# One of eight channel tiles of a depthwise convolution moved from TensorE tap matmuls to VectorE multiply-adds

## The chip, the cores and the metric

The kernel runs on one core of a Trainium2 chip. A core has five engines with a queue of instructions each: TensorE (PE; the loading of its stationary operand is shown apart, as PEld), VectorE (DVE), ScalarE (ACT), GpSimd (POOL) and SyncE (SP), which here only issues DMAs. Engines run independently; within one queue the order is fixed when the kernel is built, and an instruction that waits holds up what stands behind it. The metric is the device time of one execution in microseconds (us). Of the kernel before, three runs gave 2607.24, 2607.55 and 2607.57 us: median 2607.55.

## The reference, cut to what matters

The program is an encoder of four layers over 512 positions and 1024 channels, in float32. Layers 0 and 3 mix positions with a convolution module, layer 1 with neighbourhood attention, layer 2 with retention; a gated conv-FFN follows each. Only the convolution module is touched:

```python
def conv_module(h, w_in, b_in, dw_w, dw_b, ln_g, ln_b, w_out):
    a, gt = jnp.split(h @ w_in + b_in, 2, axis=-1)
    u = a * jax.nn.sigmoid(gt)
    u = dwconv(u, dw_w, dw_b)
    u = layernorm(u, ln_g, ln_b)
    return jax.nn.silu(u) @ w_out
```

`dwconv` is depthwise, 31 taps wide and centred: output position t of channel c is the bias of c plus the sum over k = 0..30 of `dw_w[k, c] * u[t + k - 15, c]`, with zeros beyond the ends. No channel sees another, so each of the eight tiles of 128 channels can be made in its own way. The layernorm behind it needs mean and variance over all 1024 channels of a position.

## The kernel before

**Precision.** Every product is made on TensorE from a high and a low part (`split`, L163, and `split_w`, L146: ScalarE casts the high part to fp32r, VectorE subtracts it from the source to get the low part). A matrix product is three matmuls, high by high, high by low, low by high (`mm3`, L153, its matmuls at L154 to L156).

**Layout.** The residual stream lies as 8 tiles `x[k]` of 128 channels by 512 positions. Weights are streamed: SP issues the load of a raw tile `wr`, then it is split into `wh` and `wl` (three buffers each). PSUM has eight banks; the convolution takes four as pool `psa` (the two input products) and four as `psb` (the taps and the transposes).

**The convolution** (`conv`, L349) runs per channel tile m = 0..7.

- `front(m)` (L370) makes the two halves of the input product, 48 matmuls; VectorE scales both by the row norm (L392, L394), ScalarE applies the sigmoid (L393), and VectorE writes the gated product `u` (L396), de-interleaved by position modulo 4 into one of two tiles `us`. POOL then issues four copies (L401), which gather 32 channels by 4 position phases onto 128 partitions as `xf`; `split` makes `X` from it (high and low).
- `taps(m, X, half)` (L406) makes 64 of the 128 channels as two blocks of 32. Per block a banded matrix of the tap weights `wraw` of 576 KB is loaded by SP (L413), split into `W` (three buffers; ScalarE L164, VectorE L165), and 9 pairs of matmuls follow: one 256 columns wide (L419) and one 128 wide (L422). A channel tile has four blocks, so 36 pairs. VectorE adds bias and both parts into `y` (L431, L434), which lies by position on the partitions and by channel along the free axis.
- Four groups of `bn_stats` (`BNG`, L63, L439), each issued when the last of its channels is there, gather the layernorm's statistics; behind the last of them 23 matmuls whose result is not used stand on TensorE (L444), then `norm(k)` (L469) normalises `y`, transposes it back (L482) and the output product follows.

**Order.** The program is written as a software pipeline (L448): step m traces `front(m)`, then the second half of tile m - 2's taps, then the first half of tile m - 1's. The text is not the final order. A planner simulates all engines with a cost estimate for each instruction and gives each queue its order from that; where several instructions are ready, the earlier-traced one goes first, as far as the trace shows. In the steady part TensorE runs 40 front matmuls, three tap blocks, 8 front matmuls, one tap block, and so on. What sets when something can run is therefore its data and buffers, then its place in the text.

**Start.** For the first convolution the weights of `front(0)` (input tiles 0 and 8) are loaded with the input `x`, in parts (L989), and its two banks come from `psb`.

Of the kernel before, what the change touches and what calls it, by code (L numbers as in the profile page):

```python
# [8 lines left out]
F32 = mybir.dt.float32  # L9
# [8 lines left out]
P = 128  # L18
T = 512
# [4 lines left out]
CW = 31  # L24
FT = 22
FC = 3
# [6 lines left out]
_n = 0  # L33
for _name, _w in (
    ("n1g", 32), ("n2g", 32), ("cbin", 32), ("clg", 16), ("clb", 16), ("qg", 1), ("kg", 1), ("gng", 16), ("logd", 8),
    ("fdw", 4 * 44 * FC), ("fdb", 4 * 44),
):
    COLS[_name] = _n
    _n += _w
# [11 lines left out]
SH = 4  # L51
# [8 lines left out]
NRAW = 2  # L60
HPO = 100000
NQZ = 2
BNG = ((0, 8), (8, 14), (14, 15), (15, 16))  # L63
NWARM = 23


@with_exitstack
def tile_trunk(
# [17 lines left out]
    def nm(s):  # L86
        uid[0] += 1
        return f"{s}{uid[0]}"
# [152 lines left out]
    def stats2():  # L241
        ps = bank(psb)
        bcast(rstd_col, ps)
        nc.scalar.copy(rstd_bc, ps)
# [104 lines left out]
    def conv(j, after):  # L349
        with ExitStack() as st:  # L350
# [8 lines left out]
            with ExitStack() as s2:  # L359
                up = s2.enter_context(tc.tile_pool(name=nm("cvu"), bufs=1, reuse_waits=RW))  # L360
                dp = s2.enter_context(tc.tile_pool(name=nm("cvd"), bufs=2, reuse_waits=RW))
                us = [up.tile([P, SH, QL], F32, tag=f"u{i}", name=nm("u")) for i in range(2)]
                for u in us:
                    nc.vector.memset(u[:, :, :4], 0.0)
                    nc.vector.memset(u[:, :, QL - 4:], 0.0)
# [2 lines left out]
                    nc.vector.tensor_copy(ap, sqacc[:, :1])  # L368

                def front(m):  # L370
                    where = psb if early and m == 0 else psa
                    pa, pg = bank(where), bank(where)
                    ws = state.pop("first", None) if m == 0 else None
                    if ws:
                        for k in range(KD):
                            s = slice(k * P, (k + 1) * P)
                            for ps, (wh, wl) in zip((pa, pg), ws):
                                mm3(ps, wh[:, s], wl[:, s], xhi[k], xlo[k], k == 0, k == KD - 1)
                        after_squares(bias[:, :1])
                        nc.scalar.dma_start(bias, cdb[j])  # L380
                        stats1()
                        stats2()
                    else:
                        for (ps, c) in ((pg, m + 8), (pa, m)):
                            wh, wl = load_w(cw_in[j, c], D)
# [3 lines left out]
                            if m == 0:  # L389
                                stats2() if c == 0 else stats1()  # L390
                    ta, tg = t512(), t512()
                    nc.vector.tensor_tensor(tg, pg, rstd_bc, MUL)  # L392
                    nc.scalar.activation(tg, tg, AF.Sigmoid, bias=pc("cbin", j * 16 + 8 + m))  # L393
                    nc.vector.tensor_tensor(ta, pa, rstd_bc, MUL)  # L394
                    u = us[m % 2]
                    state["u"] = nc.vector.scalar_tensor_tensor(  # L396
                        u[:, :, 4:4 + P], ta.rearrange("p (q s) -> p s q", s=SH),
                        pc("cbin", j * 16 + m), tg.rearrange("p (q s) -> p s q", s=SH), ADD, MUL)
                    xf = dp.tile([P, 4, QL], F32, tag="xf", name=nm("xf"))
                    for b in range(4):  # L400
                        nc.gpsimd.dma_start(xf[:, b, :], u[32 * b:32 * b + 32])  # L401
                    X = dp.tile([P, 4, 2, QL], F32R, tag="X", name=nm("X"), bufs=3)
                    split(xf, X[:, :, 0, :], X[:, :, 1, :])
                    return X

                def taps(m, X, half):  # L406
                    ps = bank(psb)
# [25 lines left out]
                            bb[:, b].unsqueeze(1).broadcast_to([P, SH, nb, 32]), ADD)  # L433
                        nc.vector.tensor_tensor(yv[:, :, b], pv[:, 0, :, b], t[:, :, b], ADD)  # L434
                    c1 = m * 2 + half + 1
                    for n, (a0, a1) in enumerate(BNG):
                        if c1 == a1:
                            for r in range(SH):
                                nc.vector.bn_stats(bst[:, r, n, :], y[:, r, a0 * 64:a1 * 64])  # L439
                    if c1 == 16:  # L440
# [4 lines left out]
                        with tc.issue_after(state["cast"].ins):  # L445
                            nc.scalar.activation(sm(1), zero, AF.Silu)

                fr = {}  # L448
                for m in range(10):
                    if m < 8:  # L450
                        fr[m] = front(m)
                    if m >= 2:
                        taps(m - 2, fr[m - 2], 1)
                    if 1 <= m <= 8:
                        taps(m - 1, fr[m - 1], 0)
            mv = sm(8)
            for r in range(SH):
                nc.vector.bn_aggr(mv[:, 2 * r:2 * r + 2], bst[:, r])
# [579 lines left out]
def _layout(inp):  # L1038
# [28 lines left out]
    put("logd", np.repeat(f["ret_log2_inv_decay"].reshape(1, 8), P, 0))  # L1067
    put("fdw", f["ffn_dw_w"].reshape(4, FC, 44, P).transpose(3, 0, 2, 1).reshape(P, -1))
    put("fdb", cols(f["ffn_dw_b"]))

    half = 128
    theta = (np.float32(1.0) / (np.float32(10000.0) ** np.linspace(0.0, 1.0, half, dtype=np.float32))).astype(np.float32)
# [71 lines left out]
```

## Time and profile before

| what | value |
|---|---|
| median of three runs | 2607.55 us |
| the profiled execution's own time | 2606.53 us |
| its span, first to last instruction | 2604.8 us |
| mean granted TensorE clock | 1.000 |
| busy: PE / PEld / DVE / ACT / POOL | 2591.2 / 2154.2 / 1641.6 / 1052.8 / 235.0 us |
| first convolution, first front to last taps and norm | about 20 to 172 us of the span |
| second convolution, the same | about 2021 to 2180 us |

Busy time of an engine is the union of its instructions' records, so that matmuls that overlap in the pipeline are counted once; their mean duration is longer than the distance from one to the next. The chain of waits is followed back from the last instruction to what released each step. In a group of instructions the columns are line, engine, operation, output <- inputs by the program's names, shapes and count; then busy us and mean ns of one; then idle us of the engine just before them and what ended it. In a table by stretch of time an engine's busy us stands with its count of instructions in brackets.

### The profile page before, as it was taken

The numbers are of one execution on the slowest core, as the hardware profiler recorded it, in microseconds if no ns is written. First come the engines' busy times: TensorE is split into PE (matmuls) and PEld (weight loads), VectorE is DVE, ScalarE is ACT, GpSimd is POOL, SyncE is SP. The second block draws the span as 40 slices with busy tenths as digits, with TensorE's granted clock in tenths as the row PEclk, the third lists the DMA queues.
The fourth block names the chain that finished last, engine by engine and source line by source line (L and its number), as shares of the span: only waits on it lengthen the run. The fifth ranks groups of instructions, "written<-read, shape, count | busy, mean of one in ns | idle before, by whom it ended". The sixth has DMA issues, their size and how long they took to land.

```text
span 2604.8 us, 32584 instructions
## 1 busy us (share of the span) xinstructions
PE 2591.2 (99%) x12886; PEld 2154.2 (83%) x12886; DVE 1641.6 (63%) x2640; ACT 1052.8 (40%) x1431; POOL 235.0 (9%) x253
## 2 busy tenths in 40 slices
PE   9999999999999999999999999999999999999999
PEld 7988888889998888888888888888888888788888
DVE  6777777437878777634656566677733667677732
ACT  5444444335655444323333333444422445444421
POOL 1104000003421100000000000100000101100000
PEclk9999999999999999999999999999999999999999
DMA  6624222333232222333221221222233651222232
GB/s 235 222 92 162 90 96 96 90 98 117 82 93 82 97 93 93 93 97 109 73 89 65 89 73 65 97 98 89 95 91 110 228 192 69 92 97 96 89 109 79
DMA packets 79785, 275.12 MB, mean 106 GB/s; under 512 B 10080, under 2 KB 13024, under 8 KB 79632
## 3 DMA queue, kind: packets, MB, share of 16 engines
q1 hardware_dynamic: 74304, 259.18, 30.5%
q0 software_dynamic: 4032, 11.14, 1.5%
q10 hardware_dynamic: 1296, 2.72, 0.3%
q8 instruction: 101, 1.65, 0.3%
q14 instruction: 52, 0.43, 0.1%
HBM read 263.04 MB, written 5.63 MB: 103 GB/s over the span
## 4 chain that ended last, share of the span: by engine, by line
PE 98%; DVE 1%; DMA 1%; ACT 0%; issue 0%; POOL 0%; SPq 0%; DVEq 0%; POOLq 0%
PE ps L155 27%; PE ps L154 27%; PE ps L156 27%; PE ps L419 3%; PE ps L160 3%; PE ps L161 3%; PE ps L159 3%; PE ps L422 1%; PE ps L311 1%; PE ps L312 1%; PE ps L316 1%; PE ps L664 1%; PE ps L444 0%; DMA x<-in_xT 0%; PE ps L482 0%
## 5 line engine op out<-in xcount | busy, mean ns | idle before, releaser
L149 ACT CAST wh<-wr 128x1024 fp32r<-128x1024 f32 (+1 forms) x410 | 424.1, 1036 | 1083.8 <-PE ps L155 791.0
L155 PE MATMUL ps<-xl,wh 128*128 128x512 f32 x1856 | 736.4, 397 | 0.3 <-DVE xl L213 0.3
L156 PE MATMUL ps<-xh,wl 128*128 128x512 f32 x1856 | 733.4, 395 | 0.1
L154 PE MATMUL ps<-xh,wh 128*128 128x512 f32 x1856 | 730.8, 394 | 1.7 <-DVE t L392 1.1
L150 DVE TENSOR_TENSOR wl<-wr,wh 128x1024 fp32r<-128x1024 f32 (+1 forms) x407 | 494.9, 1216 | 337.9 <-ACT wh L149 335.3
L154 PEld LDWEIGHTS ps<-xh,wh 128*128 128x128 f32 x1856 | 348.4, 188 | 88.9 <-DVE t L392 1.3
L155 PEld LDWEIGHTS ps<-xl,wh 128*128 128x128 f32 x1856 | 348.5, 188 | 83.9 <-DVE xl L213 0.6
L156 PEld LDWEIGHTS ps<-xh,wl 128*128 128x128 f32 x1856 | 348.3, 188 | 81.7 <-DVE wl L150 0.5
L154 PE MATMUL ps<-hh,wh 128*128 128x512 f32 (+1 forms) x726 | 281.7, 388 | 0.5 <-DVE x L341 0.5
L155 PE MATMUL ps<-hl,wh 128*128 128x512 f32 (+1 forms) x726 | 281.6, 388 | 0.0
L156 PE MATMUL ps<-hh,wl 128*128 128x512 f32 (+1 forms) x726 | 281.6, 388 | 0.0
L277 DVE TENSOR_TENSOR t<-ps,rstd_bc 128x512 f32<-128x512 f32 x176 | 120.9, 691 | 158.5 <-PE ps L156 158.5
L231 POOL TENSOR_TENSOR sqacc<-t,sqacc 128x512 f32<-128x512 f32 x49 | 75.2, 1534 | 1261.9 <-ACT t L226 1261.4
L154 PEld LDWEIGHTS ps<-hh,wh 128*128 128x128 f32 x726 | 136.5, 188 | 31.3 <-DVE x L341 0.7
L155 PEld LDWEIGHTS ps<-hl,wh 128*128 128x128 f32 x726 | 136.5, 188 | 30.7
L156 PEld LDWEIGHTS ps<-hh,wl 128*128 128x128 f32 x726 | 136.5, 188 | 30.6
L160 PE MATMUL ps<-wl,xh 128*128 128x256 f32 (+1 forms) x512 | 159.2, 312 | 0.6 <-DVE wl L150 0.6
L161 PE MATMUL ps<-wh,xl 128*128 128x256 f32 (+1 forms) x512 | 159.2, 312 | 0.0
L159 PE MATMUL ps<-wh,xh 128*128 128x256 f32 (+1 forms) x512 | 158.5, 312 | 0.0
L280 ACT ACTIVATE t<-t,par 128x512 f32<-128x512 f32 x176 | 142.7, 815 | 6.0 <-DVE t L277 5.9
L284 DVE SCALAR_TENSOR_TENSOR t<-t,par,t 128x511 f32<-128x511 f32 x176 | 132.2, 751 | 5.5
L419 PE MATMUL ps<-W,X 128*128 128x256 f32 x576 | 134.2, 331 | 0.9 <-DVE W L165 0.9
(236 smaller groups left out, 3481.9 us busy)
## 6 DMA issues: line engine op xcount, KB each, us to landing
wr<-in_f_up SPq DMA_DIRECT2D x176, 512.0 KB, 3.3
wraw<-in_cdw SPq DMA_DIRECT2D x64, 576.0 KB, 4.7
wr<-in_f_down SPq DMA_DIRECT2D x64, 448.0 KB, 3.3
wr<-in_f_down SPq DMA_DIRECT2D x32, 512.0 KB, 3.5
wr<-in_cw_in SPq DMA_DIRECT2D x30, 512.0 KB, 4.0
wr<-in_nat_qkv SPq DMA_DIRECT2D x24, 512.0 KB, 3.3
wr<-in_cw_out SPq DMA_DIRECT2D x16, 512.0 KB, 3.4
wr<-in_ret_qk SPq DMA_DIRECT2D x16, 512.0 KB, 3.3
```

The costliest lines, as they stand in the source:

```text
L149: nc.scalar.copy(hi[:, :n], raw[:, :n])
L150: eng.tensor_tensor(lo[:, :n], raw[:, :n], hi[:, :n].bitcast(F32), SUB)
L154: nc.tensor.matmul(o, wh, ah, start=first, stop=False)
L155: nc.tensor.matmul(o, wh, al, start=False, stop=False)
L156: nc.tensor.matmul(o, wl, ah, start=False, stop=last)
L159: nc.tensor.matmul(o, ah, wh, start=first, stop=False)
L160: nc.tensor.matmul(o, ah, wl, start=False, stop=False)
L161: nc.tensor.matmul(o, al, wh, start=False, stop=last)
L277: nc.vector.tensor_tensor(u, ps, rstd_bc, MUL)
L280: nc.scalar.activation(a, u, AF.Identity, bias=pc("fdb", l * 44 + c), scale=pt[:, w + 1:w + 2])
L284: nc.vector.scalar_tensor_tensor(a[:, :T - 1], u[:, 1:], pt[:, w + 2:w + 3], a[:, :T - 1], MUL, ADD)
L419: nc.tensor.matmul(o, X[:, b, 0, a:a + P], W[:, a].rearrange("p h n -> p (h n)"), start=a == 0, stop=False)
```

## The change

Channel tile 6 (`CD`) of each of the two convolutions gets another way from `u` to `y`.

- Its gated product is written dense, with 15 zero columns on either side, into a new tile `ud`. It needs no copies by POOL and no `X`.
- `direct(k0, k1)` makes the taps on VectorE: for k = 0 one `tensor_scalar` (times the weight, plus the bias), then 30 `scalar_tensor_tensor` (`ud` shifted by k, times the weight of tap k, plus `yd`, in place). Weights and bias come as one column each from the parameter table `par`, which grows by 64 columns.
- When all 31 are traced, four TensorE transposes with a stride of four positions turn `yd` into the layout of `y`, and ScalarE copies them there.
- The order of the tiles becomes 6, 0, 1, 2, 3, 4, 5, 7, so tile 6 goes first. `CTAPS` spreads the 31 instructions over the steps of the pipeline: 0, 3, 5, 5, 5, 5, 5, 3, 0, 0. The taps of the other seven tiles start one step later, in step 2, and there is one tile fewer of them.
- What was tied to tile 0 as the first front (early weights, banks, statistics) is tied to tile 6, and the second group of `bn_stats` (channels 512 to 895) is issued behind tile 5's taps.

```diff
-BNG = ((0, 8), (8, 14), (14, 15), (15, 16))
+BNG = ((0, 8, 8), (8, 14, 12), (14, 15, 15), (15, 16, 16))
 NWARM = 23
+CD = 6
+CORDER = (CD, 0, 1, 2, 3, 4, 5, 7)
+CTAPS = (0, 3, 5, 5, 5, 5, 5, 3, 0, 0)
...
+                ud = up.tile([P, T + CW - 1], F32, tag="ud", name=nm("ud"))
+                yd = up.tile([P, T], F32, tag="yd", name=nm("yd"))
+                nc.vector.memset(ud[:, :CW // 2], 0.0)
+                nc.vector.memset(ud[:, T + CW // 2:], 0.0)
...
-                    where = psb if early and m == 0 else psa
+                    where = psb if early and m == CD else psa
...
+                    if m == CD:
+                        nc.vector.scalar_tensor_tensor(
+                            ud[:, CW // 2:CW // 2 + T], ta, pc("cbin", j * 16 + m), tg, ADD, MUL)
+                        return None
                     u = us[m % 2]
...
+                def direct(k0, k1):
+                    for k in range(k0, k1):
+                        w = pc("cwd", j * CW + k)
+                        if k == 0:
+                            nc.vector.tensor_scalar(yd, ud[:, :T], w, pc("cbd", j), MUL, ADD)
+                        else:
+                            nc.vector.scalar_tensor_tensor(yd, ud[:, k:k + T], w, yd, MUL, ADD)
+                    if k0 < k1 == CW:
+                        ps = bank(psb)
+                        yr = yd.rearrange("p (q r) -> p r q", r=SH)
+                        for r in range(SH):
+                            nc.tensor.transpose(ps[:, r * P:(r + 1) * P], yr[:, r], ident)
+                        nc.scalar.copy(y[:, :, CD * P:(CD + 1) * P],
+                                       ps.rearrange("p (r c) -> p r c", r=SH))
...
-                fr = {}
-                for m in range(10):
-                    if m < 8:
-                        fr[m] = front(m)
-                    if m >= 2:
-                        taps(m - 2, fr[m - 2], 1)
-                    if 1 <= m <= 8:
-                        taps(m - 1, fr[m - 1], 0)
+                fr, done = {}, 0
+                for n in range(10):
+                    if n < 8:
+                        fr[n] = front(CORDER[n])
+                    direct(done, done + CTAPS[n])
+                    done += CTAPS[n]
+                    if n >= 3:
+                        taps(CORDER[n - 2], fr[n - 2], 1)
+                    if 2 <= n <= 8:
+                        taps(CORDER[n - 1], fr[n - 1], 0)
...
-        for c in (0, 8):
+        for c in (CD, CD + 8):
```

More of the change, by code (lines that the diff above doesn't have):

```diff
@@ L35 @@
     ("n1g", 32), ("n2g", 32), ("cbin", 32), ("clg", 16), ("clb", 16), ("qg", 1), ("kg", 1), ("gng", 16), ("logd", 8),
-    ("fdw", 4 * 44 * FC), ("fdb", 4 * 44),
+    ("fdw", 4 * 44 * FC), ("fdb", 4 * 44), ("cwd", 2 * CW), ("cbd", 2),
 ):
@@ L370, in front @@
                 def front(m):
-                    where = psb if early and m == 0 else psa
+                    where = psb if early and m == CD else psa
                     pa, pg = bank(where), bank(where)
-                    ws = state.pop("first", None) if m == 0 else None
+                    ws = state.pop("first", None) if m == CD else None
                     if ws:
@@ L388, in front @@
                                 mm3(ps, wh[:, s], wl[:, s], xhi[k], xlo[k], k == 0, k == KD - 1)
-                            if m == 0:
-                                stats2() if c == 0 else stats1()
+                            if m == CD:
+                                stats2() if c == m else stats1()
                     ta, tg = t512(), t512()
@@ L394, in front @@
                     nc.vector.tensor_tensor(ta, pa, rstd_bc, MUL)
+                    if m == CD:
+                        nc.vector.scalar_tensor_tensor(
+                            ud[:, CW // 2:CW // 2 + T], ta, pc("cbin", j * 16 + m), tg, ADD, MUL)
+                        return None
                     u = us[m % 2]
@@ L435, in taps @@
                     c1 = m * 2 + half + 1
-                    for n, (a0, a1) in enumerate(BNG):
-                        if c1 == a1:
+                    for n, (a0, a1, at) in enumerate(BNG):
+                        if c1 == at:
                             for r in range(SH):
@@ L1069, in _layout @@
     put("fdb", cols(f["ffn_dw_b"]))
+    cd = slice(CD * P, (CD + 1) * P)
+    put("cwd", f["conv_dw_w"][:, :, cd].transpose(2, 0, 1).reshape(P, -1))
+    put("cbd", f["conv_dw_b"][:, cd].T)
     half = 128
```

## The prediction

> **What bounds the kernel now.** I read the page first: busy times and the chain of waits.
>
> ```profile
> span 2604.8 us, 32584 instructions
> ...
> PE 2591.2 (99%) x12886; PEld 2154.2 (83%) x12886; DVE 1641.6 (63%) x2640; ACT 1052.8 (40%) x1431; POOL 235.0 (9%) x253
> ...
> PE 98%; DVE 1%; DMA 1%; ACT 0%; issue 0%; POOL 0%; SPq 0%; DVEq 0%; POOLq 0%
> ```
>
> TensorE sets the end: 98% of the chain, and only 13.6 us of the span without it. Work taken from TensorE is therefore worth its full time, unless TensorE then waits. Whether it would is a matter of the two stages touched, so next I read the table by stretch: both convolutions, then one steady period of the second (48 front matmuls and 36 tap pairs).
>
> ```profile
> core 0: us, PE busy (x) PEld busy (x) DVE busy (x) ACT busy (x) POOL busy (x), PEclk, DMA share, GB/s
> ...
> 20.00:172.00 152.00, 150.86 (x943) 134.04 (x943) 109.76 (x173) 68.79 (x71) 17.46 (x32) 1.00 0.60 202
> ...
> 2021.00:2180.00 159.00, 158.06 (x974) 139.77 (x973) 109.13 (x165) 68.53 (x71) 17.41 (x32) 1.00 0.55 183
> ```
>
> ```profile
> 2084.40:2103.87 19.47, 19.47 (x123) 17.29 (x122) 12.49 (x14) 7.99 (x8) 2.16 (x4) 1.00 0.59 189
> ```
>
> TensorE is busy throughout at a granted clock of 1.00, VectorE for 72% (109.76 of 152) and 64% of the period. That is the room into which the change puts work. The waits of TensorE, first convolution and then second, each show one that concerns fronts or taps:
>
> ```profile
> PE ps L154 <- DVE t L392: 1.1, 1, 1.1
> ```
>
> ```profile
> PE ps L419 <- DVE W L165: 0.9, 1, 0.9
> ```
>
> The second is the tail: tile 7, the last, has to go through product, copies and splits before its taps. The chain in order of time shows it:
>
> ```profile
> 2152.39 0.70 DVE t L394
> ...
> 2153.18 1.16 DVE u L396
> ...
> 2154.62 1.62 POOL xf L401 x3
> 2156.25 1.91 issue
> ...
> 2158.17 4.28 DMA xf<-u
> ...
> 2162.47 0.66 ACT X L164
> ...
> 2163.80 0.42 DVE y L434
> 2164.22 1.37 DVE W L165
> ...
> 2165.63 0.38 PE ps L419
> ```
>
> From 2152.39 to 2165.63 TensorE lives on six tap blocks of earlier tiles (12.4 us by the price below), then waits.
>
> **Removed from TensorE.** At the end of the first convolution TensorE makes ten tap blocks in one run:
>
> ```profile
> 145.26:165.94 20.68, 20.68 (x90) 16.77 (x89) 1.00 0.29 97
> ...
> 145.26:165.94 20.68, 19.91 (x90) 17.21 (x90) 1.00 0.29 97
> ```
>
> These are the records of L419 and of L422 in that stretch, 90 each, so 10 blocks of 9 pairs in 20.68 us, 2.07 us each. A tile has four: 8.27 us. Two convolutions: **-16.54 us**. The mean durations on the page overlap in the pipeline and can't be added up:
>
> ```profile
> L419 PE MATMUL ps<-W,X 128*128 128x256 f32 x576 | 134.2, 331 | 0.9 <-DVE W L165 0.9
> ```
>
> **Added to TensorE.** Four transposes per convolution. The chain has a run of 16 in the retention stage; the group of L482 has their duration one by one:
>
> ```profile
> 1320.51 1.75 PE ps L890 x16
> ```
>
> ```profile
> L482 PE MATMUL ps<-ident,yn 128*128 128x128 f32 x64 | 11.2, 279 | 0.1
> ```
>
> 1.75 / 16 = 0.109 us each in a run, so 8 of them cost 0.87 us. The new ones read their source with a stride of four positions, which no row shows: from 0.109 if the load still hides behind the matmul ahead, to 0.279 each (2.23 in all) if none overlaps. I take 0.109, the pace of a run, as they too stand in one: **+0.87 us**. Net -15.67.
>
> The Trainium skill ("TensorE: Matmul & The Clock Gate", Part 4: PE-mode transpose) puts a transpose at about 275 ns in the context of a kernel, most of it access latency. The row's 279 ns agrees as a duration, but the run of 16 shows that it is not the distance between two. By the page's figure the eight would cost 2.2 us, and the net would be -14.3.
>
> **Added to VectorE.** Per convolution 31 instructions over 512 elements. Their likeness is the FFN's pair that adds a shifted tile times a column into an accumulator in place:
>
> ```profile
> 402.69 0.75 DVE L282 SCALAR_TENSOR_TENSOR t<-t,par,t 128x511 f32<-128x511 f32 x1
> 403.47 0.75 DVE L284 SCALAR_TENSOR_TENSOR t<-t,par,t 128x511 f32<-128x511 f32 x1
> ```
>
> The second needs the first's result and starts 0.78 us after it. So 31 x 0.78 = 24.2 us per convolution; the first of them, a `tensor_scalar`, has no row of its form and is priced alike (0.8 us or less, it moves nothing).
>
> **Removed from VectorE**, by the groups of the steady period and of the first convolution:
>
> ```profile
> L165 DVE TENSOR_TENSOR W<-wraw,W 128x1152 fp32r<-128x1152 f32 x4 | 5.4, 1358 | 1.2 <-ACT W L164 1.2
> ...
> L396 DVE SCALAR_TENSOR_TENSOR u<-t,par,t 128x512 f32<-128x512 f32 x1 | 1.1, 1141 | 0.1
> L434 DVE TENSOR_TENSOR y<-ps,t 128x256 f32<-128x256 f32 x2 | 0.8, 425 | 0.1
> L431 DVE TENSOR_TENSOR t<-ps,bias 128x256 f32<-128x256 f32 x2 | 0.8, 422 | 0.3 <-PE ps L422 0.3
> L165 DVE TENSOR_TENSOR X<-xf,X 128x544 fp32r<-128x544 f32 x1 | 0.7, 718 | 0.0
> ...
> L394 DVE TENSOR_TENSOR t<-ps,rstd_bc 128x512 f32<-128x512 f32 x1 | 0.7, 692 | 3.5 <-PE ps L156 3.5
> ```
>
> Four `W` splits (5.4), one `X` split (0.7), two evacuations into `y` (1.7), and the dense product in place of the de-interleaved one (1.14 to 0.75, as L282): 8.2 us. Net +16.0, so in the first convolution 109.76 + 16.0 = 125.8 us in 152 - 7.8 = 144.2 us: **87%**. A steady period gets five of them, 12.49 + 3.9 = 16.4 of 19.47. VectorE doesn't become the bound by its sum.
>
> **Whether it comes late.** What TensorE needs of VectorE in time is `W`, with three buffers: when a block ends, ScalarE casts the next but two and VectorE splits it, while TensorE has two blocks left, 4.14 us.
>
> ```profile
> L164 ACT CAST W<-wraw 128x1152 fp32r<-128x1152 f32 x64 | 73.9, 1159 | 64.6 <-PE ps L422 58.8 <-issue 2.9 <-DMA wraw<-in_cdw 2.3
> ```
>
> 1.16 + 1.36 = 2.52 us, so a slack of 1.6 us. One or two of the new instructions ahead of a split (0.78, 1.56) cost nothing; three cost 0.7 us, five 2.3 us. They wait for nothing but `ud` and their predecessor, so the planner can put them into VectorE's idle stretches from the first front on (3.5 us before each L394 in the period above): the first convolution's stretch has 152 - 109.76 = 42.2 us idle, and the net of 16.0 is wanted. I expect them to be done well before their last place in the text.
>
> **The ends.** Start: tile 0's `X` is now that of the second front. Before, in the first convolution, VectorE's rows at the start were:
>
> ```profile
> 38.20 0.68 DVE L394 TENSOR_TENSOR t<-ps,rstd_bc 128x512 f32<-128x512 f32 x1
> ...
> 52.20 0.73 DVE L165 TENSOR_TENSOR X<-xf,X 128x544 fp32r<-128x544 f32 x1 [1.31 <-ACT X L164]
> ```
>
> ```profile
> 52.85 0.28 PE L419 MATMUL ps<-W,X 128*128 128x256 f32 x1
> ```
>
> The second `X` was split by 52.9 us, and TensorE, with fronts until then, took its first tap at 52.85. A fourth front can now stand there, since the second's banks were read by 38.9 us. Nothing is lost. Tail: between the last front and tile 7's taps stood (5,1), (6,0), (6,1), now (4,1), (5,0), (5,1): six blocks as before, so the wait of 0.9 us stays. In the first convolution the same chain had little left:
>
> ```profile
> 154.91 0.72 DVE L165 TENSOR_TENSOR X<-xf,X 128x544 fp32r<-128x544 f32 x1 [0.36 <-ACT X L164]
> 155.55 0.42 DVE L434 TENSOR_TENSOR y<-ps,t 128x256 f32<-128x256 f32 x1
> 155.96 2.63 DVE L165 TENSOR_TENSOR W<-wraw,W 128x1152 fp32r<-128x1152 f32 x2
> ```
>
> Tile 7's first `W` was ready at 155.96 + 1.36 = 157.3, wanted at 145.26 + 6 x 2.07 = 157.7. One new instruction in front there would cost 0.4 us, in the second convolution 0.8; a few more in the middle may cost some tenths. For all waits together I take **+1.0 us**, between -2.0 (both waits of before vanish) and +4.2 (three in a row, 0.7 us, in six of the twelve periods).
>
> **At no cost.** ScalarE loses four casts of `W` and one of `X` (5.3 us) and gets one copy out of PSUM; POOL loses four copies and SP four loads of 576 KB; none sets the end. The copy's likeness:
>
> ```profile
> L244 ACT COPY rstd_bc<-ps 128x512 f32<-128x512 f32 x7 | 4.1, 584 | 6.6 <-PE ps L190 6.6
> ```
>
> It holds up a cast behind it by 0.6 us, inside the slack of 1.6; without that cover it costs 0.6 us per convolution. The four `bn_stats` of the second group keep their place among the taps. The 64 columns more of `par` (33 KB, beside 576 KB of each load saved) lie behind `x` on SP's queue, and the first that reads anything of that load is the sigmoid of the first front, once the row norm is there.
>
> **The sum.** 2606.53 (the profiled execution's own time) - 16.54 + 0.87 + 1.0 = 2591.9. The median stands 1.0 above the profiled run: **2592.9 us**, range of this case alone -2.0 to +4.2 in place of +1.0: 2589.9 to 2596.1. By the skill's price of the transposes it would be 2594.2.
>
> **Rivals.**
>
> *Splits come late, by a little.* The planner reckons the new instructions too cheap or groups them by three ahead of a `W` split in every period: 12 x 0.7 = 8.4 us of waits. 2607.55 - 15.67 + 8.4 = 2600.3 us. For it: VectorE at 87% serves in fixed order. Against: the slack, and the idle stretches during the fronts' 11 us.
>
> *The cover of the tail goes.* TensorE, with less work, uses up two of the six blocks before the last front is through, and waits 4.14 us for tile 7's `X` in each convolution: +8.3, 2600.2 us. For it: 0.4 us left there and 0.9 missing. Against: the count of blocks is the same, and fronts stand ahead of taps in the text.
>
> *Slower: the groups of `CTAPS` go as they are traced,* five in a row (3.9 us) ahead of a split that TensorE needs next, because they stand before that step's taps in the text. Each costs 2.3 us, a group of three 0.7: per convolution 5 x 2.3 + 2 x 0.7 = 12.9, in all 25.8: 2617.7 us. The point from which it is slower: 7.8 us of waits per convolution, that is 1.3 us in each of six periods, or four in a row each time. Against: the first groups are ready while TensorE runs fronts alone, and the chain once begun needs no wait.
>
> That the change doesn't do what it says I see no way for: 72 of 576 pairs are not issued.
>
> **How the numbers follow.** Forecast 0.70; splits a little late 0.11; tail 0.08; groups as traced 0.11. A measurement tells no change from about 0.2%, 5.2 us, so no change is 2602.3 to 2612.8. The forecast, the tail and 0.08 of the small delays are faster: 0.86. No change: 0.03 of the small delays and 0.04 of the groups' milder part: 0.07. Slower: 0.07. Range: 2589 (a little under the case's lower end, as orders elsewhere may shift) to 2601, which takes in both middle rivals and leaves out about 0.16.
>
> **What would show it.** Right: 504 records of L419's successor for 576, TensorE's busy time down by 15 to 16 us, each convolution shorter by 6.5 to 8.5 us, the new instructions 0.75 us long and the last of them before the last front's end, and waits of TensorE for `W` and `X` under 4 us in all. Transposes in a row at 0.11 us. Wrong: waits for `W` once per period, or tile 7's taps starting over 1.5 us after the sixth block; new instructions well over 0.8 us; VectorE over 95% busy in the convolutions; or a change of more than 3 us outside them.

## The result, and the profile after

| | before | after |
|---|---|---|
| median | 2607.39 us (2606.79 to 2607.57, 4 runs) | 2589.45 us (2588.89 to 2590.25, 4 runs) |
| profiled execution's own time | 2606.53 us | 2588.89 us |
| its span | 2604.8 us | 2586.8 us |

The ratio is 0.9932, with a 95% interval of 0.9919 to 0.9944: 17.9 us less, where the forecast had 14.7 less. The page of the kernel after, with the span and the busy times:

```profile
span 2586.8 us, 32299 instructions
...
PE 2575.8 (100%) x12750; PEld 2138.5 (83%) x12750; DVE 1664.1 (64%) x2688; ACT 1041.4 (40%) x1423; POOL 229.9 (9%) x245
```

TensorE is busy 15.4 us less, and the span is 18.0 us shorter: TensorE not only has less to do, it also waits less. VectorE has 22.5 us more and still isn't the bound. From the table of groups after (L445 is the successor of L419, and L423 holds the 30 multiply-adds of each convolution):

```profile
L445 PE MATMUL ps<-W,X 128*128 128x256 f32 x504 | 117.6, 331 | 0.0
...
L423 DVE SCALAR_TENSOR_TENSOR yd<-ud,par,yd 128x512 f32<-128x512 f32 x60 | 44.9, 748 | 0.5
```

There are 72 fewer tap pairs, and the 0.9 us that L419 waited for `W` has become 0.0. Next, the chain of waits in order of time shows where the gain lies. The first row of each pair is a run of four transposes at the start of the convolution (the row norm), the second the 23 matmuls behind the last taps. Before:

```profile
25.06 0.44 PE ps L183 x4
...
166.10 5.32 PE ps L444 x23
...
2023.59 0.44 PE ps L183 x4
...
2174.36 5.30 PE ps L444 x23
```

After, with one of the two runs of the new transposes (L428):

```profile
24.73 0.44 PE ps L186 x4
...
135.53 0.47 PE ps L428 x4
...
156.71 5.31 PE ps L470 x23
...
2014.60 0.44 PE ps L186 x4
...
2156.32 5.31 PE ps L470 x23
```

From the norm to the 23 matmuls the first convolution took 141.04 us before and takes 131.98 after, the second 150.77 and 141.72: 9.06 and 9.05 us less. The 18.04 us by which the last row stands earlier are these, 0.33 us at the start (25.06 to 24.73; in the runs below this row lies between 24.8 and 26.3, in `two_tiles` near 22, so 0.33 us can't be put down to the change), less 0.40 us that come back between the convolutions. The waits of TensorE in the first convolution after:

```profile
PE ps L157 <- ACT sh L167: 0.9, 1, 0.9
PE ps L157 <- ACT wh L152: 0.2, 1, 0.2
```

In the second only the first of these lines is there. Both were there before too and are not waits for taps (the first belongs to the output product behind the convolution, the second to the very first front). The 1.1 us for `t` and the 0.9 us for `W` are gone. Last, the table by stretch, for the two convolutions (columns as in the prediction):

```profile
20.00:162.50 142.50, 142.46 (x874) 125.92 (x872) 120.56 (x194) 63.66 (x67) 15.28 (x28) 1.00 0.59 197
2012.00:2162.00 150.00, 149.95 (x906) 131.99 (x905) 120.65 (x187) 63.40 (x67) 15.19 (x28) 1.00 0.53 174
```

TensorE misses 0.04 and 0.05 us in 292.5 us, at a clock of 1.00. VectorE is at 120.56 / 142.5 = 85% in the first. How it fits the new work in, the timeline of VectorE shows (start, duration, line) in a steady period of the second convolution, and after it the range of all 60:

```profile
2080.20 0.74 DVE L423 SCALAR_TENSOR_TENSOR yd<-ud,par,yd 128x512 f32<-128x512 f32 x1
2080.86 1.35 DVE L168 TENSOR_TENSOR W<-wraw,W 128x1152 fp32r<-128x1152 f32 x1
2082.13 0.42 DVE L457 TENSOR_TENSOR t<-ps,bias 128x256 f32<-128x256 f32 x1
```

```profile
L423 DVE SCALAR_TENSOR_TENSOR yd<-ud,par,yd x60: 736/746/768, 44.1 to 2084.7; 128x512 f32<-128x512 f32 x60
```

They stand singly or in small groups between the splits, from 44.1 us on. In the first convolution the last is done at 113.2 us, 22 us before the transposes that read it (135.53), in the second at 2085.5, some 50 us before them (2135.16). A multiply-add lasts 0.74 us, but what stands behind it starts 0.66 us after it (2080.20 to 2080.86).

### The profile page after: what moved, and what is told of

It reads as the page before. It is cut to its first block, busy times and chain, and to the rows that moved or that the text cites. A ratio compares the mean times of both kernels' runs of the same rounds, so it can differ in the third digit from the quotient of the medians.

```text
span 2586.8 us, 32299 instructions
## 1 busy us (share of the span) xinstructions
PE 2575.8 (100%) x12750; PEld 2138.5 (83%) x12750; DVE 1664.1 (64%) x2688; ACT 1041.4 (40%) x1423; POOL 229.9 (9%) x245
## 4 chain that ended last, share of the span: by engine, by line
PE 98%; DVE 1%; DMA 0%; ACT 0%; issue 0%; SPq 0%; DVEq 0%
PE ps L157 27%; PE ps L158 27%; PE ps L159 27%; PE ps L445 3%; PE ps L163 3%; PE ps L164 3%; PE ps L162 3%; PE ps L448 1%; PE ps L314 1%; PE ps L315 1%; PE ps L319 1%; PE ps L692 1%; PE ps L470 0%; DMA x<-in_xT 0%; PE ps L510 0%; PE ps L918 0%
## 5 line engine op out<-in xcount | busy, mean ns | idle before, releaser
L283 ACT ACTIVATE t<-t,par 128x512 f32<-128x512 f32 x176 | 142.5, 814 | 6.7 <-DVE t L280 6.6
L287 DVE SCALAR_TENSOR_TENSOR t<-t,par,t 128x511 f32<-128x511 f32 x176 | 132.2, 751 | 5.6
L285 DVE SCALAR_TENSOR_TENSOR t<-t,par,t 128x511 f32<-128x511 f32 x176 | 131.1, 746 | 0.0
```

The costliest lines, as they stand in the source:

```text
L283: nc.scalar.activation(a, u, AF.Identity, bias=pc("fdb", l * 44 + c), scale=pt[:, w + 1:w + 2])
L285: nc.vector.scalar_tensor_tensor(a[:, 1:], u[:, :T - 1], pt[:, w:w + 1], a[:, 1:], MUL, ADD)
L287: nc.vector.scalar_tensor_tensor(a[:, :T - 1], u[:, 1:], pt[:, w + 2:w + 3], a[:, :T - 1], MUL, ADD)
```

## The experiments

Three theories stood at the start. *The forecast's:* TensorE's taps are worth their full time, VectorE's work is hidden, and the waits change by a little. *The place:* the gain hangs on which tile it is and where it stands in the order, for what cover TensorE keeps at the end. *The order on VectorE:* the gain hangs on the planner, which puts the multiply-adds where nobody waits. Times between the norm's row and the 23 matmuls are given as "first" and "second" below (before: 141.04 and 150.77 us; after: 131.98 and 141.72).

### The order alone

Tile 6 goes first, but its taps stay on TensorE and begin in step 1, as before.

```diff
-BNG = ((0, 8), (8, 14), (14, 15), (15, 16))
+BNG = ((0, 8, 8), (8, 14, 12), (14, 15, 15), (15, 16, 16))
+CORDER = (CD, 0, 1, 2, 3, 4, 5, 7)
...
-                        fr[m] = front(m)
+                        fr[m] = front(CORDER[m])
                     if m >= 2:
-                        taps(m - 2, fr[m - 2], 1)
+                        taps(CORDER[m - 2], fr[m - 2], 1)
```

> The new order of the channel tiles alone (6, 0, 1, 2, 3, 4, 5, 7), with tile 6 made by tap matmuls like the others and the software pipeline as before. The changed kernel lost both waits of TensorE (1.1 us in the first convolution, 0.9 in the second) on top of the matmuls. Theory A, the waits went because the taps start one step later and TensorE has a fourth front in hand: the order alone changes nothing, 2607.4 us within 1 us, and the wait of 1.1 us is there. Theory B, the order of the tiles made the waits go: 2605.4 us, and no wait for VectorE in either convolution. The wait of 0.9 us in the second came from 1.9 us between POOL's third and fourth copy of tile 7; POOL issues as many copies here as before, so if that gap hangs on the place in POOL's queue it is there again.

Measured: 2606.24 us against 2607.00, ratio 0.9997 (0.9987 to 1.0007). The waits of TensorE, one from each convolution:

```profile
PE ps L156 <- DVE t L394: 1.1, 1, 1.1
```

```profile
PE ps L421 <- DVE W L167: 1.0, 1, 1.0
```

Both waits of before are still there. So the order by itself gains nothing, and the waits went with something else in the change.

### The taps left out, in the old order

The tap matmuls of tile 6 aren't issued and nothing is put in their place (its part of `y` is zeros, so the convolution lacks these 128 channels); the order stays 0 to 7.

```diff
+                nc.gpsimd.memset(y[:, :, CD * P:(CD + 1) * P], 0.0)
...
-                    if m >= 2:
+                    if m >= 2 and m - 2 != CD:
                         taps(m - 2, fr[m - 2], 1)
-                    if 1 <= m <= 8:
+                    if 1 <= m <= 8 and m - 1 != CD:
                         taps(m - 1, fr[m - 1], 0)
```

> The kernel before, in its old order, with the tap matmuls of tile 6 left out and nothing in their place (its part of y is set to zero once by POOL, so this part of the convolution is not computed). It measures the removal alone. Forecast's price: 2 x 8.27 = 16.5 us, so 2590.9 us if the two waits stay, 2588.9 if they go. If taps of a tile were partly cover for TensorE that it would otherwise wait through (the rival of the tail's cover), clearly less is gained: 2595 or more. VectorE has 2 x 8.2 us less to do here, not more.

Measured: 2605.23 us, ratio 0.9993 (0.9984 to 1.0002). The same 72 pairs are gone, nothing is added, and of 16.5 us hardly 2 arrive. The waits of TensorE, first convolution and then second:

```profile
PE ps L420 <- ACT X L165: 3.8, 1, 3.8
```

```profile
PE ps L420 <- DVE bst L440: 4.5, 1, 4.5
```

Tile 6's four blocks stood between the last front and tile 7's taps. Without them only two blocks are left as cover for product, copies and splits of tile 7, and TensorE waits for its `X`. (The second row names `bst`, but ScalarE's cast of `X` ended at 2160.43 us and the first tap came at 2160.49.) That is not all: the table by stretch right behind the second wait shows

```profile
2160.49:2166.74 6.25, 6.25 (x28) 5.99 (x28) 1.04 (x2) 1.50 (x2) 0.00 (x0) 0.50 0.00 0
2166.74:2172.06 5.32, 5.32 (x47) 5.32 (x47) 2.48 (x7) 1.14 (x2) 0.00 (x0) 1.00 0.01 3
```

For 6.25 us the granted clock is 0.50: 28 matmuls, 14 pairs at 0.45 us, then 47 in 5.32 us, 0.23 us a pair. That costs 14 x 0.22 = 3.1 us more. The second convolution took 148.93 us, 1.84 less than before instead of 8.27: of the missing 6.4 us the longer wait explains 4.5 - 0.9 = 3.6, the clock some 3.1. The Trainium skill ("TensorE: Matmul & The Clock Gate", HAM oscillation) gives about 3.4 us as the longest idle gap that leaves the clock up. After 3.8 and 4.5 us it fell here. But shorter gaps don't always leave it up: in `two_on_vector` (below) it fell behind a wait of 1.5 us, so there the measurement and the page differ.

So the same saving is worth 2 us here and 18 us in the new arrangement, where six blocks are left as cover.

### The multiply-adds left out

Of 31 multiply-adds only the first is made (so tile 6's channels get one tap of 31); everything else is the kernel after.

```diff
                             nc.vector.tensor_scalar(yd, ud[:, :T], w, pc("cbd", j), MUL, ADD)
-                        else:
-                            nc.vector.scalar_tensor_tensor(yd, ud[:, k:k + T], w, yd, MUL, ADD)
```

> The changed kernel with 30 of the 31 multiply-adds left out in each convolution (only the first tap is computed), all else as it is. It measures what VectorE's new work costs. Theory: nothing, since TensorE waits for none of it: 2589.4 us within 0.7 us, and VectorE's busy time in each convolution down from 120.6 to about 98 us. Rival, the 87 per cent load of VectorE costs TensorE some tenths in each period: 2586 to 2588 us.

Measured: 2589.76 us (2588.80 to 2590.76), ratio 0.9934 (0.9919 to 0.9948), the time of the kernel after. First 131.89, second 141.72 us. The 45 us of multiply-adds cost nothing that can be measured. VectorE is busy for 101.86 us in the stretch of the first convolution in place of 120.56, where 98 was expected: 30 multiply-adds take 18.7 us of it, 0.62 each.

### The groups forced behind `u` and ahead of the splits

Each group of `CTAPS` has to stand behind its step's `u`, and that step's `W` splits behind the group.

```diff
-                        with tc.issue_after(state["u"].ins) if early and m * 4 + b < 5 else ExitStack():
+                        with tc.issue_after(state["d"].ins):
                             split(raw, W[:, :, 0, :], W[:, :, 1, :])
...
-                    direct(done, done + CTAPS[n])
+                    with tc.issue_after(state["u"].ins) if n else ExitStack():
+                        direct(done, done + CTAPS[n])
```

> The changed kernel with VectorE's order forced: each step's group of multiply-adds (3, 5, 5, 5, 5, 5, 3) stands behind that step's gated product and ahead of the W splits of that step's taps, so five in a row, as the text has them. It is the slower rival's placement. By the rival's price (slack 1.6 us, five cost 2.3, three 0.7): 12.9 us per convolution, 2589.4 + 25.8 = 2615.2 us, with a wait of TensorE for W in each period. Theory that TensorE's order is planned around it, front matmuls in place of taps: less than 5 us over the changed kernel in all, under 2595 us.

Measured: 2631.87 us (2631.63 to 2634.17), ratio 1.0097 (1.0082 to 1.0112): 42.4 us above the kernel after, and slower than before. The waits of TensorE in the first convolution, and two stretches of it:

```profile
PE ps L445 <- DVE W L168: 8.4, 2, 8.2
PE ps L428 <- DVE yd L423: 5.4, 1, 5.4
PE ps L157 <- DVE t L399: 2.2, 2, 1.1
```

```profile
120.00:140.00 20.00, 11.76 (x88) 11.04 (x87) 14.76 (x19) 6.94 (x7) 2.16 (x4) 0.84 0.57 182
140.00:150.00 10.00, 9.94 (x72) 9.79 (x71) 7.22 (x11) 3.50 (x4) 0.00 (x0) 0.82 0.71 236
```

The loss is real and larger than either theory had it, and of another form than the rival's: not 1 to 2 us in each period, but a few long waits (16.0 us here), and a lowered clock (0.84 and 0.82 in the two stretches); together 21.2 us in the first convolution and 20.7 in the second. So the kernel after owes its time to an order other than the text's, in which the multiply-adds run ahead of their place in it. The run holds the groups late and the splits behind them at once, and does not show which of the two costs more.

### Every multiply-add twice

A second accumulator is made with the same 31 instructions, and the transposes read both in turn. VectorE's new work is doubled, TensorE's is unchanged.

```diff
                             nc.vector.scalar_tensor_tensor(yd, ud[:, k:k + T], w, yd, MUL, ADD)
+                            nc.vector.scalar_tensor_tensor(zd, ud[:, k:k + T], w, zd, MUL, ADD)
...
-                            nc.tensor.transpose(ps[:, r * P:(r + 1) * P], yr[:, r], ident)
+                            nc.tensor.transpose(ps[:, r * P:(r + 1) * P], (zr if r % 2 else yr)[:, r], ident)
```

> The changed kernel with VectorE's new work doubled: every multiply-add is made twice, into two accumulators with the same value, and the transposes read both. Leaving the 30 multiply-adds out cost or gained nothing, so the question is where the room ends. In the changed kernel VectorE is busy for 120.6 of the first convolution's 142.5 us; 31 more at 0.75 us make 143.5. Theory, VectorE's sum then sets the convolution: at least 143.5 us plus what it idles at the start and the end (some 10 us), so 10 us or more per convolution over the changed kernel, 2610 to 2625 us, with waits of TensorE for W. Rival, the planner finds room by running ahead: under 2595 us.

Measured: 2608.25 us (2607.01 to 2609.09), ratio 1.0006 (0.9996 to 1.0015): the whole gain is spent, but nearly all of it in the first convolution (150.05 us, 18.1 above the kernel after; the second has 143.05, 1.3 above). Neither theory had this: it is not 10 us in each, and not under 2595. The wait that does it, in the first, and a stretch of each convolution:

```profile
PE ps L432 <- DVE yd L425: 15.5, 1, 15.5
```

```profile
140.00:165.00 25.00, 13.44 (x95) 13.47 (x96) 19.15 (x26) 6.29 (x7) 2.16 (x4) 0.66 0.34 104
...
2060.00:2080.00 20.00, 20.00 (x124) 17.68 (x123) 20.00 (x29) 7.90 (x8) 2.16 (x4) 1.00 0.47 149
```

In the second convolution VectorE is busy for 20.00 of 20 us and TensorE still doesn't wait in that stretch: what it needs comes in time (its one wait for VectorE, for tile 7's `X`, is 1.0 us). In the first the transposes are the trouble. They have a fixed place in TensorE's queue, VectorE isn't through by then, and everything behind them waits, 15.5 us and then at a lowered clock. So the room on VectorE is real, and what runs out first is the date of the transposes. The first convolution has less room: VectorE's work was the same in both in the kernel after (120.56 and 120.65 us), but between the norm and the 23 matmuls the first is 9.7 us shorter (131.98 against 141.72). That this is why only the first fails is argued, not shown.

### Two tiles, with help from POOL

Tiles 6 and 5 go to VectorE in both convolutions; to make room, POOL takes the `wl` subtractions of the input weights (and there is one `t` buffer fewer).

```diff
-CORDER = (CD, 0, 1, 2, 3, 4, 5, 7)
-CTAPS = (0, 3, 5, 5, 5, 5, 5, 3, 0, 0)
+CE = 5
+CORDER = (CD, CE, 0, 1, 2, 3, 4, 7)
+CTAPS = (0, 6, 12, 12, 12, 12, 8, 0, 0, 0)
...
-                            wh, wl = load_w(cw_in[j, c], D)
+                            wh, wl = load_w(cw_in[j, c], D, nc.gpsimd)
```

> Two channel tiles (6 and 5, both ahead of the others) made by multiply-adds on VectorE, and to make room for them the low parts of the input weights (16 subtractions per convolution, 1.22 us each on VectorE) made by POOL, where one was seen to take 2.40 us. One buffer fewer of 512-wide temporaries. VectorE: 120.6 + 15.2 - 19.6 = 116 us in about 134.5 us, 86 per cent, as in the changed kernel. Theory, TensorE's sum sets the end as long as VectorE has room: another 2 x (8.27 - 0.47) = 15.6 us, 2573.8 us. Rival, the weights' low parts come too late from POOL, or POOL's copies stand behind subtractions: 2580 us or more, with waits of TensorE for wl or X.

Measured: 2616.14 us (2615.14 to 2617.61), ratio 1.0038 (1.0024 to 1.0052): slower than before. The theory failed; the rival had the time (2580 us or more) and some of the waits (4.6 us for `X` and 2.1 for `wl` in the second convolution), but not what comes next. From the groups of the first convolution (20 to 170 us), both multiply-add forms:

```profile
L428 DVE SCALAR_TENSOR_TENSOR yd<-ud,par,yd 128x512 f32<-128x512 f32 x60 | 60.5, 1065 | 0.0
...
L426 DVE TENSOR_SCALAR yd<-ud,par 128x512 f32<-128x512 f32 x2 | 5.2, 2658 | 0.0
```

The same instruction that took 748 ns takes 1065 on average here, and the `tensor_scalar` 2658 instead of 538, about as long as one of POOL's subtractions in that stretch (2696). It isn't a general slowing: the median multiply-add takes 739 ns and the longest 3110, so single ones are stretched. TensorE waits 12.7 us for `yd` and 6.9 for `W` in the first convolution. The Trainium skill ("SBUF — State Buffer", Who interferes with whom) says that a VectorE instruction with two SBUF inputs contends with a GpSimd instruction that reads SBUF, and that a `tensor_scalar` in a mode that uses both port pairs can be shut out for a whole GpSimd instruction. The trace agrees with the first: the next run, without POOL's share, has a median of 744 ns and none above 772. The 2658 ns fit the second, though no run shows in which mode that `tensor_scalar` ran.

### Two tiles on VectorE alone, in both convolutions, and in the second only

The same two tiles, without POOL's share (and again one `t` buffer fewer); the transposes stand later in TensorE's queue, behind the taps of the step before, and the 62 multiply-adds spread over eight steps. `two_in_second`, with `ND` of (1, 2), does this in the second convolution only; its first has tile 6 alone and the groups of the kernel after.

```diff
+ND = (2, 2)
+ORDERS = ((CD, 0, 1, 2, 3, 4, 5, 7), (CD, CE, 0, 1, 2, 3, 4, 7))
+TAPS = ((0, 3, 5, 5, 5, 5, 5, 3, 0, 0), (0, 8, 8, 8, 8, 8, 8, 8, 6, 0))
...
+                                with tc.issue_after(state["mm"].ins):
+                                    nc.tensor.transpose(ps[:, r * P:(r + 1) * P], yr[:, r], ident)
```

> Two channel tiles (6 and 5) by multiply-adds on VectorE in both convolutions, nothing moved to POOL, and the transposes traced late and kept behind the taps of tile 4's first half on TensorE. In the kernel that shared the work with POOL the same multiply-add took 1065 ns in place of 748, and TensorE stood 12.7 us at the transposes. Theory A, both were the trouble: multiply-adds are back at 0.75 us and no transposes are waited for; VectorE's sum, 120.6 + 15.2 = 136 us against TensorE's 134.7, is the limit and costs 2 to 6 us per convolution: 2578 to 2584 us. Theory B, VectorE at its full load comes late everywhere: 2590 us or more.

> As the kernel with two tiles on VectorE, but only in the second convolution; the first has tile 6 alone, as in the changed kernel, with its transposes kept behind a tap block. With doubled work the first convolution lost 18.7 us and the second 1.6, so the second has room for more. Theory: the second convolution gains 7.8 us less 0 to 3, 2582 to 2585 us; rival: VectorE's load turns into waits for W, 2588 us or more.

Measured: 2592.72 us with two in both (ratio 0.9945, 0.9930 to 0.9960), and **2583.52 us** with two in the second only (2582.16 to 2585.53; ratio 0.9909, 0.9892 to 0.9925), against 2607.07 before. The deciding wait of the first kernel, in its first convolution:

```profile
PE ps L439 <- DVE yd L432: 14.0, 1, 14.0
```

and of the second kernel the wait for tile 7 and the whole stretch of the second convolution:

```profile
PE ps L460 <- DVE X L170: 1.5, 1, 1.5
```

```profile
2012.00:2155.00 143.00, 141.53 (x834) 123.71 (x833) 129.99 (x191) 59.87 (x63) 14.80 (x25) 1.00 0.51 173
```

In the first convolution of the first kernel the transposes are again too early for VectorE (140.59 us). In the second convolution of the second kernel VectorE is 91% busy (129.99 of 143) and TensorE waits 1.5 us once; this convolution takes 135.85 us, 5.9 less than in the kernel after, out of 8.27 that the second tile's taps cost. Its first takes 131.98, as there. So theory A failed in the first convolution, and theory B in the second, where TensorE isn't late everywhere.

The second convolution of `two_on_vector` has the same instructions and the same wait of 1.5 us for `X`, and takes 137.43 us, 1.6 more. The table by stretch behind that wait, first `two_on_vector` and then `two_in_second`, shows why:

```profile
2150.74:2154.25 3.51, 3.51 (x20) 3.51 (x21) 3.48 (x7) 0.45 (x1) 0.00 (x0) 0.64 0.00 0
```

```profile
2144.74:2148.00 3.26, 3.26 (x28) 3.26 (x29) 3.23 (x6) 1.06 (x1) 0.00 (x0) 1.00 0.00 0
```

In the one the granted clock falls (0.50 from 2152 to 2155 us), in the other it stays at 1.00. What decides between them is not shown.

### What became of the 0.9 us: POOL's gap

Before, POOL had paused 1.92 us ahead of tile 7's fourth copy in the second convolution; after, the four copies run through. The timeline of POOL after:

```profile
2137.44 2.16 POOL L412 DMA_DIRECT2D xf<-u  x4 [17.34 <-DVE u L407]
```

Is the pause tied to a place in POOL's instruction stream, or to a number of DMAs? `pool_shift` is the kernel before with eight instructions more on POOL that aren't DMAs; `copies_89` is the kernel after with eight copies more in the first convolution, so that POOL again issues 97 DMAs up to tile 7's fourth copy, as before (64 copies and 33 for the layer with attention), and not 89. The expectation of `copies_89` counts 89 in the kernel before, and leaves out eight of the 33; the eight copies more give the total of before all the same.

```diff
+    idle = const.tile([P, 1], F32, tag="idle", name="idle")
+    for _ in range(8):
+        nc.gpsimd.memset(idle, 0.0)
```

```diff
+                    if j == 0 and m in (1, 2):
+                        xg = dp.tile([P, 4, QL], F32, tag="xg", name=nm("xg"), bufs=1)
+                        for b in range(4):
+                            nc.gpsimd.dma_start(xg[:, b, :], u[32 * b:32 * b + 32])
```

> The kernel before, with eight tiny memsets on POOL at the very start, which nobody reads. Before, and in two kernels with as many POOL instructions, 1.9 us passed between POOL's third and fourth copy of tile 7 in the second convolution, with nothing shown that it waited for; in the changed kernel, with eight copies fewer, there is no such gap there. Theory, the gap belongs to a place in POOL's stream of instructions: it moves to earlier copies (tile 5 or 6), tile 7's four copies are issued in 2.2 us, and TensorE's wait of 0.9 us for W behind them is gone: 2606.2 us, no more than the spread of single runs. Rival, the gap belongs to the moment (what else runs at the tail): it stays at tile 7's fourth copy, and the wait too.

> The changed kernel with eight copies more on POOL's queue in the first convolution (those of tiles 1 and 2 made a second time into a buffer nobody reads), so that POOL issues 89 DMAs in all as the kernel before does, where the gap of 1.9 us stood before the 89th. Eight memsets more did not move it. Theory, the gap hangs on the count of POOL's DMAs: tile 7's fourth copy in the second convolution is again issued 1.9 us late, and TensorE waits some tenths for tile 7. Rival, it hangs on something else of the old kernel's tail: four copies in 2.2 us as in the changed kernel.

Measured: `pool_shift` 2605.42 us, ratio 0.9997 (0.9987 to 1.0006); `copies_89`, a single run, 2589.56 us. POOL's timeline in each, first `pool_shift`:

```profile
2158.20 0.56 POOL L404 DMA_DIRECT2D xf<-u  x1 [1.93 <-issue]
```

```profile
2137.80 1.62 POOL L412 DMA_DIRECT2D xf<-u  x3 [17.34 <-DVE u L407]
2141.35 0.56 POOL L412 DMA_DIRECT2D xf<-u  x1 [1.92 <-issue]
```

Eight other instructions don't move the pause; eight DMAs bring it back, ahead of the 97th. So it goes with POOL's DMAs; whether by their count or by what they carry is not separated, as the eight are copies of the same size. In `pool_shift` the wait for `W` behind it is there too, 0.5 us. But the second half of the expectation of `copies_89` missed: with the pause back, TensorE did not wait (142.08 us; the 0.4 more than after were not followed). The rows say why it could do without. Before, six blocks from 2152.39 us ended at about 2164.8 and `W` came at 2165.59. Here they begin at 2136.00, behind 0.47 us of transposes, and end at about 2148.4; `X` reaches ScalarE (2145.16) 9.59 us after VectorE begins the scaling behind the last front, instead of 10.08, and tile 7's first `W` is there at 2148.2. So the transposes themselves and a copy that landed half a microsecond sooner make up the 0.9 us. Why it landed sooner was not tried. In the kernel after both come together with the missing pause, and `X` reaches ScalarE at 2142.94 us, 7.74 after the scaling begins: there the pause's going is a gain to spare, not what the 0.9 us hung on.

## Why the prediction was right, and what was off

The forecast was 2592.9 us, the measurement 2589.45: right in sign and inside the range given (2589.0 to 2601.0), but 3.4 us below the value taken and just under the own case's range, which began at 2589.9. That it lies inside is in part luck: the 0.9 us added below the case were for shifts in orders elsewhere, and it was the waits inside the convolutions that needed them.

- **Removed from TensorE, -16.54 us: right.** 504 records for 576, and the pace of the remaining blocks is unchanged (135.53 + 0.47 to 156.71: ten blocks in 20.71 us, 2.07 each).
- **Transposes, +0.87 us: right.** Four take 0.47 us on the chain, 0.117 each, so 0.94 in all. Their weight loads do take longer with the stride (205 ns against 140 for the dense ones), but stay behind the matmul ahead.
- **VectorE's work costs nothing: right**, and for the reason given, as `no_multiply_adds` shows. Its load came to 85% where 87% was worked out, and the net of +16.0 us per convolution was too high: by the two pages it is 22.5 us for both, 11.3 each. The duration was right (746 ns), but 0.78 is the pace of two that need each other, and most stand between other instructions, at 0.66; the `tensor_scalar` took 538 ns, not 0.8 us. That they go into the idle stretches was only half right: many stand between two splits, where the slack of 1.6 us covers them. The last one stood 22 and 50 us ahead of the transposes, as the forecast had it ("well before their last place in the text").
- **Waits, +1.0 us: mis-sized; this is the term that failed.** It came out at -2.0, the lower bound. The forecast kept both waits of before and added some tenths. The step "six blocks as before, so the wait of 0.9 us stays" left out that the new transposes stand behind the last front and are cover themselves (0.47 us), and that POOL's pause, which the quoted chain showed as "1.91 issue", goes when the change takes eight of its DMAs away. `copies_89` shows that the first, with a copy that landed half a microsecond sooner, is enough. The 1.1 us in the first convolution is gone in the kernel after and with the multiply-adds left out, and still there with the order alone and with the taps left out in the old order; so it goes with what the first two share, a first tile without taps on TensorE and the later start of the others. VectorE's rows before show what held it:

```profile
57.85 0.42 DVE L431 TENSOR_TENSOR t<-ps,bias 128x256 f32<-128x256 f32 x1 [1.36 <-PE ps L422]
58.19 0.68 DVE L392 TENSOR_TENSOR t<-ps,rstd_bc 128x512 f32<-128x512 f32 x1
```

The scaling of a front (L392), for which TensorE waited, stood in VectorE's queue behind the bias of the first taps (L431), and that waits for the end of these taps. In the kernel after VectorE has three fronts' L399 done by 39.1 us (before: two L392), ahead of any tap. Which part of the change moved it was not isolated.
- **The balance.** -16.54 + 0.94 - 2.0 = -17.6. The two convolutions show -18.1; the 0.5 us between the two sums (0.16 and 0.35) were not followed. The forecast's mark "each convolution shorter by 6.5 to 8.5 us" was missed by that and the waits: 9.05.
- **The ends, "six blocks as before": right, and it decides.** The rival "the cover of the tail goes" described a mechanism that exists: in the old order it takes the saving down to 2 us. It didn't come, and the forecast's reason against it (as many blocks as before) fits that. But its price had only the wait, not the 3 us of halved clock behind it.
- **The slower rival, "the groups go as they are traced": not what happened.** Brought about by force, it gives 2631.9 us instead of 2617.7. The forecast summed small waits per period; what comes is a few long ones, the longest (8.2 and 5.4 us) followed by a lowered clock.
- **Splits late by a little:** nothing of it; TensorE misses 0.1 us in 292.5.

## What to carry to other kernels

Work taken off the engine that sets the end is worth its full time only if it wasn't the cover of something late: here it paid to make the odd tile the first one, not the one that stands between the last product and its use. Instructions of the bound engine that read a long chain elsewhere (here the transposes) have to stand late in its queue, for when they came too early everything behind them waited (15.5 and 14.0 us) and the clock fell too. A second tile paid in the second convolution (2583.5 us with two there only), and not in the first, where VectorE has the same work in 9.7 us less.

## What the runs showed of the hardware

- After a wait of TensorE of 3.8 or 4.5 us the granted clock was 0.52 and 0.50 for some 6 us, 0.45 us a pair of taps instead of 0.23: the wait of 4.5 us cost 7.6. After one of 1.5 us it fell to 0.50 for some 3 us in `two_on_vector`, and stayed at 1.00 in `two_in_second`.
- POOL paused 1.91 to 1.93 us ahead of its 97th DMA in the five kernels that have so many (before, `order_only`, `taps_left_out`, `pool_shift`, `copies_89`), eight memsets more or not. The kernels with 89 (after, `no_multiply_adds`, `groups_forced`, `doubled`) show no such pause at the copies of tile 7.
- Beside POOL's subtractions a multiply-add of 748 ns took 1065 on average (median 739, longest 3110), and a `tensor_scalar` of 538 took 2658.
- The doubled multiply-adds that stop TensorE for 15.5 us in the first convolution cost 1.3 us in the second, though VectorE is busy for 20.00 of 20 us there in the stretch shown: a busy VectorE alone doesn't tell whether TensorE waits.
- A multiply-add of 0.74 us takes 0.66 us of VectorE's time when something else stands behind it (0.62 by leaving 30 of them out), and 0.78 when the next one needs its result.
